# One order of scores and masks in windowed attention, norm roots on one engine, a longer modulation pause and one group of PSUM banks, in a two-layer backbone on one core

## The chip, the cores and the metric

The kernel runs on one core of one Trainium2 chip. The metric is the device time of the whole program in microseconds (us), the median over runs; lower is better.

## The reference, cut to what matters

The reference is a two-layer diffusion backbone over 512 latent tokens with 256 context tokens ahead of them, width 1024, all in fp32. Each layer is half a SwiGLU feed-forward step, a token mixing, and another half step; each of the three is fed by an RMSNorm modulated by shift, scale and gate, which are computed from the conditioning vectors (adaLN, nine vectors per layer, one set for the latent tokens and one for the context).

```python
def ffn_half_step(x, g, shift, scale, gate, wg, wu, wd):
    h = modulate(rmsnorm(x, g), shift, scale)
    return x + 0.5 * gate * swiglu(h, wg, wu, wd)     # widths 1024 -> 2816 -> 1024

# layer 0 mixes by spatial gating beside windowed attention, layer 1 by a recurrent block
def block(args):                      # one block of 128 queries, 8 query heads on 2 key heads
    qj, kj, vj, mj = args             # kj: the blocks before, at and after the queries
    s_loc = jnp.einsum('bqkgd,bnkd->bkgqn', qj, kj).astype(jnp.float32) * scale
    s_loc = jnp.where(mj, s_loc, NEG_INF)             # |key - query| <= 128
    s_ctx = jnp.einsum('bqkgd,bnkd->bkgqn', qj, k_ctx).astype(jnp.float32) * scale
    p = jax.nn.softmax(jnp.concatenate([s_loc, s_ctx, s_sink], axis=-1), axis=-1)
    ...
```

## The kernel before, in words

**Layout.** All activations are held transposed, features on the 128 partitions and 768 tokens (256 context, then 512 latent) along the free axis. Work on tokens goes in two halves of 384, the first and the second half below. Every fp32 product is made of three matmuls on operands split into a high and a low part (`mm3`), issued through the helper at line 121; so almost all matmuls carry the line L121 in the trace, and the tile names tell them apart: `pgu`, `pd` and `seeded` for the feed-forward products, `ps` for projections, norm sums and spreads, `sl` and `sc` for local and context scores, `pt` for transposes of the probabilities, `po` for output projections.

**What sets the order.** Instructions are emitted from Python into one stream per engine; a scheduler behind the program may still bring an instruction that is ready ahead of others of its engine. A planner (`Clock`, with `clk.at`) advances an estimated time with every matmul that is emitted and fires the events that are due: preparing weights (loads on SP's queue, splits into high and low on ScalarE and VectorE, at L198, L201, L228 and L245), the applying of norms, and steps of the modulation.

**Modulation.** `ada_event` (L521) makes one step of the adaLN product each 1.7 us of the planner's time in the first FFN, each 2.5 us in the second and each 4.8 us between them; a step is two updates on VectorE (L496) of a running sum with a loaded piece of the weights (`aw`). It pauses while `bg["on"]` is false. That is set false at L856, ahead of the last down projection of each feed-forward step, and true again when the next norm has been applied to the second half.

**Norms.** When a half of the tokens has its new residual, `stats` (L575) sums the squares with a matmul against ones, and `rsqrt` (L142) takes the reciprocal root of the sums: three VectorE instructions, then three Newton rounds on 128x3 or 128x4 elements. For a second half they run on VectorE with three instructions a round (L150, L152, L153); for a first half on GpSimd with four (L150, L155, L156, L157). `spread` then brings the roots to all partitions with a matmul against the identity, and the norm is applied feature block by feature block. Five first-half norms of this kind are waited for by TensorE: ahead of the mixing of layer 0, ahead of the second FFN of layer 0, ahead of the two FFN steps and the mixing of layer 1.

**PSUM.** The eight PSUM banks are in two groups, six (`psp`) and two (`psx`). `bank()` (L108) goes round all eight, except while `banks["six"]` is set: then it goes round the six, and the two others hold the pair of tiles that stay for a whole run of chunks (`hold`, L764). This pair belongs to the feed-forward chunks made with seven products in place of eight (`seven`, L771): the pair is seeded by copies on ScalarE (L790, L792) and added to by later products. Two chunks, gate and up, make a pair of feature blocks (`gate_up_seven`). The last group of a step makes two of these pairs and then the last down projection (L843 to L856).

**Attention.** A `Unit` is one block of 128 queries, one key head and two query heads; there are 16 over the latent tokens and 8 over the context. `weigh` (L1046) makes for each of the two heads the local scores (three matmuls on 64 rows, as a head has 64 features), then adds the masks of the window's two edges (a bf16 matmul of 128 rows against the identity per edge: one for the outer blocks, two for the inner ones), then takes the row maximum on VectorE; after both heads come the context scores of both in one bank, their maximum, and the exponentials on ScalarE. `turn` transposes the probabilities on TensorE a unit later.

Of the kernel before, what the change touches and what calls it, by code (L numbers as in the profile page):

```python
# [12 lines left out]
F32 = mybir.dt.float32  # L13
# [4 lines left out]
ALU = mybir.AluOpType  # L18
PSUM = bass.MemoryType.PSUM
DRAM = bass.MemoryType.DRAM  # L20

D = 1024
DK = 8
DFF = 2816
NCTX = 256
NX = 512
NT = NCTX + NX
# [62 lines left out]
def hybrid_kernel(ctx: ExitStack, tc: tile.TileContext, a: dict, out: bass.AP):  # L90
# [10 lines left out]
    psp = ctx.enter_context(tc.tile_pool(name="psp", bufs=6, space=PSUM))  # L101
    psx = ctx.enter_context(tc.tile_pool(name="psx", bufs=2, space=PSUM))
# [3 lines left out]
    banks = {"n": 0, "six": False}  # L106

    def bank(name="ps"):  # L108

        banks["n"] = (banks["n"] + 1) % 8  # L110
        if banks["n"] >= 6 and banks["six"]:
            banks["n"] = 0
        if banks["n"] >= 6:
            return psx.tile([128, 512], F32, tag="px", name=name)
        return psp.tile([128, 512], F32, tag="ps", name=name)
# [429 lines left out]
    class Norm:  # L545
# [29 lines left out]
        def stats(self):  # L575
            nt = self.n // 128
            ps = bank()
            for i in range(nt):
                mm(ps[:, i:i + 1], self.ssq[:, i * 128:(i + 1) * 128], ones[:, 0:1], True, True, 4)
            self.r = const.tile([128, 4], F32, tag="rstd" + self.which, name="rstd")  # L580
            rsqrt(ps[:, 0:nt], self.r[:, 0:nt], nt, 1.0 / D, self.which, dve if self.c1 == NT else pool)
# [70 lines left out]
    def ffn(l, j, halves, before, nxt, reserve=(), pre={}):  # L652
# [7 lines left out]
        with tc.tile_pool(name=f"ffn{l}{j}", bufs=4) as fp:  # L660
# [101 lines left out]
            held = {}  # L762

            def hold():  # L764

                banks["six"] = True
                for n in (6, 5):
                    held[n] = psx.tile([128, 512], F32, tag="px", name="seeded")[:, 0:384]
                    mm(held[n], hi[0][:, 0:128], hi[0][:, L], True, True)
# [54 lines left out]
            for gi, (f0, ng, dn) in enumerate(steps):  # L824
# [18 lines left out]
                if saving:  # L843
                    gate_up_seven(f0, G)
                    gate_up_seven(f0 + 2, G)
                    banks.update(six=False, n=5)
# [49 lines left out]
    def even_mixer(before):  # L896
        hi, lo = H
        xd = dp.tile([128, 8, NT], F32, name="xd")
        with ExitStack() as es:
# [140 lines left out]
            class Unit:  # L1040
# [5 lines left out]
                def weigh(self):  # L1046
# [16 lines left out]
                    S = {}  # L1063
                    if kind == "x":
                        k0, k1 = max(0, j - 1), min(4, j + 2)
                        n = (k1 - k0) * 128
                        self.kblocks += [2 + b for b in range(k0, k1)]
                        for hh in range(2):
                            ps = bank("sl")
                            scores(ps[:, 0:n], 2 * p + hh, NCTX + k0 * 128, NCTX + k1 * 128, False)  # L1070
                            edge = [(0, 0)] * (j > 0) + [(n - 128, 1)] * (j < 3)
                            for e, (o, m) in enumerate(edge):
                                mm(ps[:, o:o + 128], identb, masks[:, m], False, e == len(edge) - 1)
                            S[hh] = ps
                            dve.tensor_reduce(st[:, hh, 1:2], ps[:, 0:n], axis=mybir.AxisListType.X, op=ALU.max)
                    pc = bank("sc")
                    for hh in range(2):
                        scores(pc[:, hh * 256:hh * 256 + 256], 2 * p + hh, 0, NCTX, True)
                    dve.tensor_reduce(st[:, :, 0:1], pc.rearrange("p (h n) -> p h n", h=2), axis=mybir.AxisListType.X, op=ALU.max)
# [376 lines left out]
    for cc in range(4):  # L1456
# [4 lines left out]
        if cc == 0:  # L1461
            two = arrive(*TB)
            stream["limit"] = 8
            for i, key in enumerate(pre):
                pre[key] = bank("pre") if i < 2 else psx.tile([128, 512], F32, tag="px", name="pre")
            banks["six"] = True
# [106 lines left out]
```

## Time and profile before

| | |
|---|---|
| median of 3 runs | 2602.93 us (2600.84 to 2604.24) |
| profiled execution, its own time | 2604.11 us |
| its span in the trace | 2602.3 us |
| granted TensorE clock, mean | 0.988 of full speed |
| busy share: PE, PEld, DVE, ACT, POOL | 97%, 91%, 72%, 48%, 9% |
| DMA | 328.46 MB, mean 126 GB/s |

PE is TensorE's matmuls, PEld its weight loads (they overlap the matmuls), DVE is VectorE, ACT is ScalarE, POOL is GpSimd, SP is SyncE, which issues loads. The span is the time from the first to the last instruction of the profiled execution; all starts in the rows are microseconds from its begin. The granted clock is the share of full speed that the chip gave TensorE. A matmul's end is modelled and overlaps the start of the next, so the distance of two starts tells more of its cost than its duration.

### The profile page before, as it was taken

Reading aid. Unit: us, or ns where it says so; the run is one execution under the profiler, and the core shown is the slowest. Engines: PE = TensorE matmul, PEld = TensorE weight load, DVE = VectorE, ACT = ScalarE, POOL = GpSimd, SP = SyncE. Lnnn points to the kernel's source line nnn. Section 1 sums busy time; section 2 is a strip of 40 time slices with the busy share of each in tenths; the row PEclk is TensorE's granted clock in tenths of the full one; section 3 lists DMA queues with packets and bytes.
Section 4 is the critical chain, followed back from the end, with each engine's and each line's share of the span. In section 5 each row is a group of like instructions: output and inputs, shape, how many; then the busy total and the mean of one; then the engine's idle time right before and its main releaser. Section 6 shows DMA issues by size and latency. Waiting matters only on the chain. (4 is left out here: it accounts for less than half of the span.)

```text
span 2602.3 us, 37742 instructions
## 1 busy us (share of the span) xinstructions
PE 2534.7 (97%) x14370; PEld 2356.5 (91%) x14370; DVE 1875.2 (72%) x3635; ACT 1246.4 (48%) x2433; POOL 227.5 (9%) x329
## 2 busy tenths in 40 slices
PE   8999999999999999999999999999999999999998
PEld 5999999999899999999999889999999988988887
DVE  7987987887869697786687978745468898644444
ACT  3344444445555344444454444444545996433322
POOL 0012102200000002102220020121200000000000
PEclk9999999999999999999999999999999999999999
DMA  9357557652103416646675176554642123332221
GB/s 326 113 131 194 156 144 171 152 177 97 49 17 110 139 60 163 152 140 130 146 182 192 48 178 193 159 102 106 138 130 81 51 80 103 108 97 97 90 89 57
DMA packets 248430, 328.46 MB, mean 126 GB/s; under 512 B 19984, under 2 KB 172728, under 8 KB 247736
## 3 DMA queue, kind: packets, MB, share of 16 engines
q1 hardware_dynamic: 213264, 278.69, 33.2%
q0 software_dynamic: 34560, 47.20, 12.3%
q8 instruction: 112, 1.84, 0.3%
q14 instruction: 70, 0.57, 0.1%
q10 hardware_dynamic: 424, 0.15, 0.0%
HBM read 262.04 MB, written 63.96 MB: 125 GB/s over the span
## 5 line engine op out<-in xcount | busy, mean ns | idle before, releaser
L121 PE MATMUL pd<-ghi,w 128*128 128x256 f32 (+2 forms) x2528 | 645.7, 342 | 1.9 <-ACT ghi L135 1.8
L121 PE MATMUL pgu<-hhi,w 128*128 128x384 f32 (+2 forms) x2144 | 594.8, 349 | 0.9 <-ACT hhi L601 0.6
L121 PEld LDWEIGHTS pd<-ghi,w 128*128 128x128 f32 x2528 | 440.0, 188 | 53.9 <-ACT ghi L135 4.7
L121 PE MATMUL pd<-glo,w 128*128 128x512 f32 (+2 forms) x1264 | 431.4, 342 | 0.6 <-DVE glo L136 0.6
L121 PEld LDWEIGHTS pgu<-hhi,w 128*128 128x128 f32 x2144 | 393.0, 189 | 27.6 <-ACT hhi L601 1.3
L121 PE MATMUL pgu<-hlo,w 128*128 128x384 f32 (+2 forms) x1072 | 374.8, 350 | 1.3 <-DVE hlo L607 1.2
L201 DVE TENSOR_TENSOR w<-raw,w 128x512 fp32r<-128x512 f32 x404 | 270.5, 687 | 85.0 <-ACT w L198 79.0
L198 ACT ACTIVATE w<-raw 128x512 fp32r<-128x512 f32 x404 | 244.6, 626 | 181.9 <-PE pd L121 79.3
L496 DVE SCALAR_TENSOR_TENSOR acc<-aw,cs,acc 128x512 f32<-128x512 f32 x392 | 281.1, 745 | 56.3 <-DMA aw<-in_ada_w_dram 55.5
L696 POOL DMA_DIRECT2D kept<-add x240 | 208.9, 910 | 1184.1 <-ACT add L695 1179.2
L228 DVE TENSOR_TENSOR w<-raw,w 128x512 fp32r<-128x512 f32 x348 | 232.2, 687 | 108.2 <-ACT w L245 105.9
L121 PE MATMUL seeded<-form,w 128*128 128x384 f32 x1392 | 263.2, 336 | 5.0 <-ACT seeded L790 3.2
L121 PEld LDWEIGHTS pd<-glo,w 128*128 128x128 f32 x1264 | 237.9, 188 | 27.5 <-DVE glo L136 2.9
L695 ACT ACTIVATE add<-pd,gate 128x256 f32<-128x256 f32 x240 | 138.3, 580 | 245.6 <-PE pd L121 232.5
L121 PE MATMUL seeded<-hhi,w 128*128 128x384 f32 x928 | 247.9, 335 | 3.0 <-DVE uv L798 1.7
L121 PEld LDWEIGHTS seeded<-form,w 128*128 128x128 f32 x1392 | 244.5, 189 | 6.7 <-ACT seeded L790 3.9
L245 ACT ACTIVATE w<-raw 128x512 fp32r<-128x512 f32 x348 | 207.5, 626 | 61.7 <-DVE raw L242 20.2
L121 PEld LDWEIGHTS pgu<-hlo,w 128*128 128x128 f32 x1072 | 202.8, 189 | 15.2 <-DVE hlo L607 2.1
L121 PE MATMUL ps<-hhi,w 128*128 128x384 f32 (+1 forms) x704 | 198.3, 356 | 7.6 <-ACT t L1327 6.3
L121 PEld LDWEIGHTS seeded<-hhi,w 128*128 128x128 f32 x928 | 168.6, 188 | 5.5 <-DVE uv L798 2.7
L121 PE MATMUL seeded<-hlo,w 128*128 128x384 f32 x464 | 155.1, 335 | 0.4 <-DVE hlo L136 0.4
L121 PEld LDWEIGHTS ps<-hhi,w 128*128 128x128 f32 x704 | 132.5, 194 | 15.4 <-ACT t L1327 7.2
(304 smaller groups left out, 3655.3 us busy)
## 6 DMA issues: line engine op xcount, KB each, us to landing
aw<-in_ada_w_dram SPq DMA_DIRECT2D x128, 512.0 KB, 5.3
raw<-in_ffn_w_gate_dram SPq DMA_DIRECT2D x44, 1024.0 KB, 5.4
raw<-in_ffn_w_up_dram SPq DMA_DIRECT2D x44, 1024.0 KB, 5.3
raw<-in_ffn_w_down_dram SPq DMA_DIRECT2D x40, 1024.0 KB, 5.2
kept<-add POOLq DMA_DIRECT2D x120, 256.0 KB, 5.6
kept<-add POOLq DMA_DIRECT2D x120, 128.0 KB, 5.4
x<-kept SPq DMA_DIRECT2D x48, 192.0 KB, 4.2
fw<-in_ada_w_dram SPq DMA_DIRECT2D x16, 512.0 KB, 8.9
```

The lines of the kernel that those rows point to most:

```text
L121: pe.matmul(o, w, x, start=start, stop=stop, skip_group_check=again)
L198: act.activation(tiles[i][:, 0:512], self.raw[:, i * 512:i * 512 + 512], AF.Copy)
L201: dve.tensor_tensor(t[:, 512:1024], self.raw[:, i * 512 - 512:i * 512], t[:, 0:512].bitcast(F32), op=ALU.subtract)
L228: dve.tensor_tensor(l, src[key], h.bitcast(F32), op=ALU.subtract)
L245: act.activation(halves_of(key)[0], src[key], AF.Copy)
L496: dve.scalar_tensor_tensor(acc[:, v, :], w[:, k, :], s, acc[:, v, :], op0=ALU.mult, op1=ALU.add)
L695: act.activation(t, ps[:, 0:c1 - c0], AF.Copy, scale=state["gate"][:, 4 * c + d, v:v + 1])
L696: pool.dma_start(out=saved(l, j)[:, 4 * c + d, c0:c1], in_=t, accum_op=ALU.add)
```

## The change

In `weigh` the context scores and their maximum come first, then the local scores of both heads, then the masks of both heads with their maxima. The Newton rounds of all norms of `stats` go to VectorE. In the last group of a feed-forward step with seven-product chunks the modulation is switched off between the two pairs of feature blocks, in place of after them. The two groups of PSUM banks become one of eight, and the held pair is taken from it.

```diff
--- before.py
+++ after.py
@@ -98,20 +98,11 @@
     wp = ctx.enter_context(tc.tile_pool(name="wp", bufs=SLOTS))
     rp = ctx.enter_context(tc.tile_pool(name="rp", bufs=2))
     tp = ctx.enter_context(tc.tile_pool(name="tp", bufs=8))
-    psp = ctx.enter_context(tc.tile_pool(name="psp", bufs=6, space=PSUM))
-    psx = ctx.enter_context(tc.tile_pool(name="psx", bufs=2, space=PSUM))
+    psp = ctx.enter_context(tc.tile_pool(name="psp", bufs=8, space=PSUM))
     dp = ctx.enter_context(tc.tile_pool(name="dp", bufs=1, space=DRAM))
 
 
-    banks = {"n": 0, "six": False}
-
     def bank(name="ps"):
-
-        banks["n"] = (banks["n"] + 1) % 8
-        if banks["n"] >= 6 and banks["six"]:
-            banks["n"] = 0
-        if banks["n"] >= 6:
-            return psx.tile([128, 512], F32, tag="px", name=name)
         return psp.tile([128, 512], F32, tag="ps", name=name)
 
     def temp(name="t"):
@@ -578,7 +569,7 @@
             for i in range(nt):
                 mm(ps[:, i:i + 1], self.ssq[:, i * 128:(i + 1) * 128], ones[:, 0:1], True, True, 4)
             self.r = const.tile([128, 4], F32, tag="rstd" + self.which, name="rstd")
-            rsqrt(ps[:, 0:nt], self.r[:, 0:nt], nt, 1.0 / D, self.which, dve if self.c1 == NT else pool)
+            rsqrt(ps[:, 0:nt], self.r[:, 0:nt], nt, 1.0 / D, self.which, dve)
 
         def prep_mod(self):
             m = mod(self.l, 3 * self.j + 1)
@@ -763,9 +754,8 @@
 
             def hold():
 
-                banks["six"] = True
                 for n in (6, 5):
-                    held[n] = psx.tile([128, 512], F32, tag="px", name="seeded")[:, 0:384]
+                    held[n] = bank("seeded")[:, 0:384]
                     mm(held[n], hi[0][:, 0:128], hi[0][:, L], True, True)
 
             def seven(ch, emit):
@@ -842,8 +832,8 @@
                     continue
                 if saving:
                     gate_up_seven(f0, G)
+                    bg["on"] = False
                     gate_up_seven(f0 + 2, G)
-                    banks.update(six=False, n=5)
                     for i in range(2):
                         X[i] = xp.tile([128, 4, NT], F32, tag="x", name=f"x{i}")
                     for c0, c1 in halves:
@@ -1061,22 +1051,22 @@
 
                     self.kblocks = [0, 1]
                     S = {}
+                    pc = bank("sc")
+                    for hh in range(2):
+                        scores(pc[:, hh * 256:hh * 256 + 256], 2 * p + hh, 0, NCTX, True)
+                    dve.tensor_reduce(st[:, :, 0:1], pc.rearrange("p (h n) -> p h n", h=2), axis=mybir.AxisListType.X, op=ALU.max)
                     if kind == "x":
                         k0, k1 = max(0, j - 1), min(4, j + 2)
                         n = (k1 - k0) * 128
                         self.kblocks += [2 + b for b in range(k0, k1)]
+                        edge = [(0, 0)] * (j > 0) + [(n - 128, 1)] * (j < 3)
                         for hh in range(2):
-                            ps = bank("sl")
-                            scores(ps[:, 0:n], 2 * p + hh, NCTX + k0 * 128, NCTX + k1 * 128, False)
-                            edge = [(0, 0)] * (j > 0) + [(n - 128, 1)] * (j < 3)
+                            S[hh] = bank("sl")
+                            scores(S[hh][:, 0:n], 2 * p + hh, NCTX + k0 * 128, NCTX + k1 * 128, False)
+                        for hh in range(2):
                             for e, (o, m) in enumerate(edge):
-                                mm(ps[:, o:o + 128], identb, masks[:, m], False, e == len(edge) - 1)
-                            S[hh] = ps
-                            dve.tensor_reduce(st[:, hh, 1:2], ps[:, 0:n], axis=mybir.AxisListType.X, op=ALU.max)
-                    pc = bank("sc")
-                    for hh in range(2):
-                        scores(pc[:, hh * 256:hh * 256 + 256], 2 * p + hh, 0, NCTX, True)
-                    dve.tensor_reduce(st[:, :, 0:1], pc.rearrange("p (h n) -> p h n", h=2), axis=mybir.AxisListType.X, op=ALU.max)
+                                mm(S[hh][:, o:o + 128], identb, masks[:, m], False, e == len(edge) - 1)
+                            dve.tensor_reduce(st[:, hh, 1:2], S[hh][:, 0:n], axis=mybir.AxisListType.X, op=ALU.max)
                     if kind == "x":
                         dve.tensor_tensor(st[:, :, 0:1], st[:, :, 0:1], st[:, :, 1:2], op=ALU.max)
                     dve.tensor_tensor(st[:, :, 0:1], st[:, :, 0:1], sink8[:, h0:h0 + 2].unsqueeze(2), op=ALU.max)
@@ -1461,9 +1451,8 @@
         if cc == 0:
             two = arrive(*TB)
             stream["limit"] = 8
-            for i, key in enumerate(pre):
-                pre[key] = bank("pre") if i < 2 else psx.tile([128, 512], F32, tag="px", name="pre")
-            banks["six"] = True
+            for key in pre:
+                pre[key] = bank("pre")
         for k in ks:
             for (c, f, i), ps in pre.items():
                 mm3(ps[:, 0:384], (wg, wu)[i].w(k, f * 128, f * 128 + 128),
```

## Rows read from the trace of the kernel before

**Rows 1.** The page's part 1: busy time, share of the span, instructions per engine.
```profile
PE 2534.7 (97%) x14370; PEld 2356.5 (91%) x14370; DVE 1875.2 (72%) x3635; ACT 1246.4 (48%) x2433; POOL 227.5 (9%) x329
```

**Rows 2.** Waits of PE: what was waited for, us in total, times, longest.
```profile
PE ps L121 <- POOL rstd L157: 9.0, 5, 2.5
PE ps L121 <- ACT t L1327: 6.3, 3, 3.1
...
PE ps L121 <- DVE ssq L572: 4.5, 3, 1.5
...
PE seeded L121 <- ACT seeded L790: 3.2, 2, 2.4
```

**Rows 3.** Timeline of PE, one-mask unit: start, us, operation, tiles, shapes, [idle before].
```profile
777.33 0.38 PE L121 MATMUL sl<-kv,qh 64*128 64x256 f32 x1
...
777.67 0.28 PE L121 MATMUL sl<-kv,qh 64*128 64x256 f32 x1
777.88 0.23 PE L121 MATMUL sl<-masks,identb 128*128 128x128 bf16 x1
778.04 0.38 PE L121 MATMUL sl<-kv,qh 64*128 64x256 f32 x1
...
778.75 0.38 PE L121 MATMUL sc<-kv,qh 64*128 64x256 f32 x1
778.97 0.28 PE L121 MATMUL sc<-kv,ql 64*128 64x256 f32 x1
...
779.45 0.28 PE L121 MATMUL sc<-kv,qh 64*128 64x256 f32 x1
779.65 0.33 PE L1111 MATMUL pt<-ident,pc 128*128 128x128 f32 x1
```

**Rows 4.** Timeline of PE, a unit with two masks for each head.
```profile
741.33 0.44 PE L121 MATMUL sl<-kv,qh 64*128 64x384 f32 x1
...
742.05 0.28 PE L121 MATMUL sl<-masks,identb 128*128 128x128 bf16 x2
742.27 0.44 PE L121 MATMUL sl<-kv,qh 64*128 64x384 f32 x1
...
744.11 0.44 PE L1111 MATMUL pt<-ident,pc 128*128 128x128 f32 x2
```

**Rows 5.** Timeline of PE, the spreads of four first-half norms and one sum.
```profile
565.71 1.65 PE L121 MATMUL ps<-ident,rstd 128*128 128x128 f32 x6 [2.53 <-POOL rstd L157]
...
884.62 0.93 PE L121 MATMUL ps<-ident,rstd 128*128 128x128 f32 x6 [2.55 <-POOL rstd L157]
...
1421.74 0.80 PE L121 MATMUL ps<-ones,ssq 128*128 128x1 f32 x6 [1.48 <-DVE ssq L572]
...
1427.04 0.94 PE L121 MATMUL ps<-ident,rstd 128*128 128x128 f32 x6 [0.69 <-POOL rstd L157]
...
2210.59 1.22 PE L121 MATMUL ps<-ident,rstd 128*128 128x128 f32 x4 [2.52 <-POOL rstd L157]
```

**Rows 6.** Windows: us, busy of PE, PEld, DVE, ACT, POOL, PEclk, DMA share, GB/s.
```profile
560.00:570.00 10.00, 7.47 (x38) 7.15 (x37) 5.54 (x13) 2.60 (x5) 3.62 (x12) 0.83 0.17 52
```

**Rows 7.** Timeline of POOL, begin of the first root's Newton rounds.
```profile
561.13 0.19 POOL L150 TENSOR_TENSOR rs<-rstd 128x3 f32<-128x3 f32 x1 [77.71 <-DVE rstd L148]
```

**Rows 8.** Timeline of DVE, begin and end of two second-half Newton chains.
```profile
911.77 0.15 DVE L150 TENSOR_TENSOR rs<-rstd 128x3 f32<-128x3 f32 x1
...
917.46 0.15 DVE L153 SCALAR_TENSOR_TENSOR rstd<-rs,rstd 128x3 f32<-128x3 f32 x1
...
1449.50 0.16 DVE L150 TENSOR_TENSOR rs<-rstd 128x3 f32<-128x3 f32 x1
...
1451.07 0.16 DVE L153 SCALAR_TENSOR_TENSOR rstd<-rs,rstd 128x3 f32<-128x3 f32 x1
```

**Rows 9.** Timeline of DVE, a modulation update before the third norm.
```profile
1416.06 0.75 DVE L496 SCALAR_TENSOR_TENSOR acc<-aw,cs,acc 128x512 f32<-128x512 f32 x1 [1.89 <-DMA aw<-in_ada_w_dram]
```

**Rows 10.** Tile aw: engine, operation, duration ns (min/median/max), first and last start.
```profile
L496 DVE SCALAR_TENSOR_TENSOR acc<-aw,cs,acc x392: 724/745/755, 43.4 to 1667.7; 128x512 f32<-128x512 f32 x196
```

## The prediction

> **What bounds the kernel.** I read the page's part 1 first: TensorE is busy 2534.7 of 2602.3 us, 97% of the span, VectorE 72%, ScalarE 48%, GpSimd 9% [rows 1]. TensorE is the bound, and an edit is worth what it takes from TensorE's own work or from the 67.6 us in which it stands idle. Then the waits of TensorE [rows 2]: the longest group is the norm's reciprocal root on GpSimd, 9.0 us in 5 waits; the sums of squares on VectorE add 4.5 us in 3, the gate sigmoids of the odd mixer 6.3 us in 3, the seeding of the held banks 3.2 us in 2. Last the timelines at the lines that the diff touches, and there the windows, since a gap can cost more than itself: in the 10 us around the first root the granted clock is 0.83 [rows 6]. The levels are 2.4 and 1.2 GHz, so 0.17 of 10 us, 1.7 us of work, is lost on top of the wait. Three of the five gaps have such a window (0.83 each, after waits of 2.53, 2.55 and 2.52 us [rows 5]); the two short ones of 0.7 us have not.
>
> **Scores in a row, masks behind them (attention).** There are 16 units over x (4 blocks, 2 key heads, 2 pairs). Before, TensorE does: scores of head 0, its masks, scores of head 1, its masks, context scores of both, then transposes. The scores use 64 rows of the array, masks and transposes 128. The starts in [rows 3] show what a change costs. Within one kind a 256-column matmul takes 0.12 us: the first three scores start at 777.33 and the third at 777.67, so 0.34 for two, and after a mask the first takes 0.22 (778.75 to 778.97); 0.34 less 0.22 is 0.12. The score ahead of a mask takes 0.21 (777.67 to 777.88), that ahead of the transposes 0.20 (779.45 to 779.65): 0.09 extra each. A lone mask takes 0.16 (777.88 to 778.04), two in a row 0.22 [rows 4], so a mask followed by a mask takes 0.06 and one followed by a score 0.10 more. The score after the mask has 0.10 extra too.
> After the change a unit has the 6 context scores, 6 local scores, then 2 or 4 masks, then the transposes. Removed: two entries into masks less the one that stays (0.09), two exits from masks to scores (2 x 0.20), and the exit from scores to transposes (0.09): 0.58 us. Added: the last mask to the transposes, which no row shows. The bounds are 0 (like mask to mask) and 0.10 (like mask to score). So 0.48 to 0.58 per unit; I take 0.53, times 16 = 8.5 us. The unit's block of 2.32 us (777.33 to 779.65), and 2.78 us with two masks per head (741.33 to 744.11 [rows 4]), should become about 1.8 and 2.25.
> In the Trainium skill, "TensorEngine Tiling (Array Packing)", section Key Properties, says that a change of tiling mode, not of the tile, drains TensorE. The trace agrees for 64 to 128 rows, and no run here shows the mask to transpose step; by that rule it would not drain, as both have 128 rows, and the term would be 16 x 0.58 = 9.3 us.
> What hides the rest: the row maxima move. The context maximum comes first, and the two local ones end the block, so the exponentials of a unit start some 0.3 us later; its transposes come only after the next unit's scores and filling matmuls, a unit later (12 us here: three units lie between 741.33 and 777.33 [rows 3, 4]), so TensorE does not see it. Lower bound of the term: the instructions are put in order by a scheduler that may slip other work between the masks; half of it, 4 us.
>
> **Norm roots on VectorE.** Five first-half norms change engine; each loses 12 GpSimd instructions and gains 9 on VectorE. On GpSimd the first chain runs from 561.13 [rows 7] to TensorE's start at 565.71 [rows 5]: 4.6 us. On VectorE a bare chain takes 1.73 us (1449.50 to the end at 1451.23 [rows 8]); with another instruction in every gap 5.84 us (911.77 to 917.61 [rows 8]). These are the two ends: 2.9 us earlier than now, or 1.3 later. Behind the chain on VectorE stand the residual updates and sums of the second half, delayed by 9 x 0.2 = 1.8 us at most; they have that much idle time. Nothing else waits on GpSimd's queue: its accumulating DMAs are all issued by then.
> First norm (565.71): the modulation pauses there after the change, so the bare end is nearer. The wait of 2.53 and the slow clock of 1.7 go, 4.2. But the operands that the next stage reads start only as much earlier as the spread ends: 565.71 + 1.65 = 567.36 becomes 563.18 + 0.93 = 564.11 (0.93 from the second spread [rows 5]), 3.25. I take 3.2.
> Second (884.62, out projection): no pause, so modulation can fill the gaps; the nearest rows are the filled chain, 30 us later [rows 8]. Its eight fillers, five modulation steps and three weight preparations, cost (5.84 - 1.73) / 8 = 0.51 us each. With the five alone the chain takes 4.3 against 4.6: 0.3 gained, the clock still lost. Bounds 4.2 gained to 1.3 lost.
> Third (1427.04) and fourth (what is left of the 9.0, 0.7 too): no modulation near, bare chain: 0.7 each.
> Fifth (2210.59): no modulation is left, but weight preparations fill some gaps; with three, 1.73 + 3 x 0.51 = 3.3 against 4.6: 1.3 gained, a wait of 1.2 stays. The wait of 1.48 at 1421.74 [rows 5] left the clock whole, so the 1.7 go too: 3.0. Bounds 1.3 lost to 4.2 gained.
>
> **Pause of the modulation.** It now stops one pair (two chunks, about 29 us) before the last down projection. Before the third norm a modulation step waits 1.89 us for its DMA at 1416.06 with the updates queued behind it [rows 9], and TensorE then waits 1.48 us for the sum of squares at 1421.74 [rows 5]; the fourth norm, when modulation is over, has no such wait. So 1.5 gained; at worst 0, if the update that follows is late anyway. Some 17 steps in the first FFN (one per 1.7 us) and 12 in the second (one per 2.5) move later, with their loads on SP's queue; the last step moves from 1667.7 [rows 10] by about 29 x 2.5 = 73 us to 1740, 200 us ahead of the fourth norm and in a stretch where VectorE has room. In the pair itself VectorE's work only shrinks. No norm comes to wait for its modulation.
>
> **One group of banks.** Eight banks go round in either form and held banks leave six; I count zero. Bounds: the 6.3 us of sigmoid waits [rows 2] gained, or a new wait at each held pair (a rival).
>
> Sum: 8.5 + 3.2 + 0.3 + 0.7 + 0.7 + 3.0 + 1.5 = 17.9 us. The profiled execution took 2604.1 us (span 2602.3, the rest lies around it and stays), 1.2 above the median of 2602.9. So 2586.2 for the profile and **2585.0 us** as median. A measurement of this kernel can tell about 0.2%, 5.2 us, from no change.
>
> **Rivals.**
> Filled chains: VectorE's order puts modulation steps, whose data were loaded before the pause, into every gap of the chain. For it: the chain from 911.77. Against: the bare one from 1449.50 [rows 8]. Price: 1.3 lost at the first, second and third, the fourth and fifth as forecast: 8.5 + 1.5 - 3.9 + 0.7 + 3.0 = 9.8, so 2593.1. Chance 0.17.
> The masks do not stay together: at the first x units the timeline shows scores of two units and products interleaved. Then 0 to 4 of the 8.5 are left: 2589.5 to 2593.5. Chance 0.08, that of a change that doesn't do what it says.
> Slower: the held pair shares the group with all others, so the banks that a chunk's first two products take are no longer apart from the seeded ones, and a product waits for an evacuation. There are 58 such chunks (18, 20, 20). Its price is the wait per chunk; the seeding wait averages 1.6 us where it occurs [rows 2]. From 0.31 us per chunk, 17.9 us in all, it eats the whole gain; at 0.6 it gives 2585.0 + 34.8 = 2619.8. For it: this wait exists. Against: it occurs twice in 58, and six free banks are the number as before. Chance 0.06.
>
> **How the numbers follow.** Forecast 0.65 (2578 to 2592), filled chains 0.17, masks apart 0.08, slower 0.06, sigmoid waits also gone 0.04 (2585.0 - 6.3 = 2578.7). Best ends of the terms (masks 16 x 0.58): 9.3 + 3.2 + 4.2 + 1.4 + 4.2 + 1.5 = 23.8, so 2579.1; half of the masks' term with filled chains: 9.8 - 4.5 = 5.3, so 2597.6. Range 2577 to 2598. Faster by more than 0.2% means below 2597.7: the forecast, the sigmoid case, most of masks apart and filled chains: 0.87. Same 0.07, slower 0.06.
>
> **What would show it.** Right: blocks of 1.8 and 2.25 us per unit; no wait of TensorE for GpSimd's root, chains under 4 us on VectorE, clock 1.00 around the first and fifth spread; no wait on the sum of squares ahead of the third norm; last modulation step after 1700 us. Wrong: a wait of TensorE on a VectorE root of 2 us or more at a first half, masks apart from each other, or new waits at the seeded banks.

## The result, and the profile after

The changed kernel took 2579.87 us in the median of 4 runs (2577.0 to 2584.91), the kernel before 2601.89 us in 4; the ratio is 0.9918, with a 95% interval of 0.9899 to 0.9936. That is 22.0 us less, where 17.9 were forecast. The profiled execution took 2580.57 us, with a span of 2578.8 us.

Part 1 of the page after; it answers to [rows 1]:

```profile
PE 2522.0 (98%) x14370; PEld 2354.4 (91%) x14370; DVE 1883.5 (73%) x3680; ACT 1247.0 (48%) x2433; POOL 210.2 (8%) x269
```

GpSimd has 60 instructions less (five norms by twelve) and VectorE 45 more (five by nine), as the diff says. TensorE's busy time fell by 12.7 us and its idle time from 67.6 to 56.8 us.

Waits of TensorE after, to be read against [rows 2]:

```profile
PE ps L112 <- ACT t L1317: 6.3, 3, 3.1
...
PE ps L112 <- DVE ssq L563: 4.4, 4, 1.6
PE ps L112 <- DVE red L497: 3.5, 1, 3.5
...
PE seeded L112 <- ACT seeded L780: 2.6, 1, 2.6
PE pt L1101 <- ACT pc L1080: 2.5, 2, 1.4
...
PE pt L1101 <- DVE rs_z L141: 2.2, 1, 2.2
...
PE ps L112 <- DVE rstd L144: 1.0, 1, 1.0
```

No wait for GpSimd's root is left, and one of 1.0 us for VectorE's. The sigmoid waits stand as they were. The wait for a modulation sum (`red`) in the first 120 us was 0.7 us before and is 3.5, and transposes, which waited once for 0.9 us, wait three times for 4.7 in all.

Timeline of TensorE after, the two kinds of unit; it answers to [rows 3, 4]:

```profile
743.30 0.39 PE L112 MATMUL sc<-kv,qh 64*128 64x256 f32 x1
...
745.28 0.40 PE L112 MATMUL sl<-masks,identb 128*128 128x128 bf16 x4
745.51 0.28 PE L1101 MATMUL pt<-ident,pc 128*128 128x128 f32 x1
...
777.44 0.38 PE L112 MATMUL sc<-kv,qh 64*128 64x256 f32 x1
...
778.86 0.28 PE L112 MATMUL sl<-kv,qh 64*128 64x256 f32 x1
779.07 0.29 PE L112 MATMUL sl<-masks,identb 128*128 128x128 bf16 x2
779.19 0.28 PE L1101 MATMUL pt<-ident,pc 128*128 128x128 f32 x1
```

The blocks take 2.21 us (743.30 to 745.51) and 1.75 us (777.44 to 779.19); before they took 2.78 and 2.32. The two masks take 0.12 us up to the first transpose, 0.06 each, so going from a mask to a transpose costs nothing. The Trainium skill ("TensorEngine Tiling (Array Packing)", Key Properties) says that a change of the tiling mode, and not of the tile alone, drains TensorE. By that rule the step from mask to transpose is free and a unit saves 0.58 us; the trace agrees, with 0.57.

Timeline of TensorE after, spreads of first-half norms, and two waits of the second halves; it answers to [rows 5]:

```profile
567.72 0.83 PE L112 MATMUL ps<-ident,rstd 128*128 128x128 f32 x6
...
588.69 1.44 PE L112 MATMUL ps<-ones,ssq 128*128 128x1 f32 x6 [1.58 <-DVE ssq L563]
...
879.39 0.83 PE L112 MATMUL ps<-ident,rstd 128*128 128x128 f32 x6
...
909.17 0.94 PE L112 MATMUL ps<-ident,rstd 128*128 128x128 f32 x6 [0.95 <-DVE rstd L144]
...
1409.87 0.83 PE L112 MATMUL ps<-ident,rstd 128*128 128x128 f32 x6
...
2189.66 0.71 PE L112 MATMUL ps<-ident,rstd 128*128 128x128 f32 x4
```

None of the first halves' spreads waits (the fourth, at 1939.50, doesn't either). Behind the first norm there is a wait that was not there before, of the second half's sum at 588.69. TensorE's order differs here: 3192 matmuls stand ahead of the sum in this trace and 3212 in the trace of before, so it comes 20 matmuls sooner.

Windows after, behind the first norm (columns as in [rows 6]):

```profile
585.00:595.00 10.00, 7.89 (x26) 6.98 (x27) 7.21 (x28) 1.43 (x3) 0.00 (x0) 0.52 0.74 239
```

The slow clock of the first norm is not gone, it came later: 0.52 in these 10 us. The instructions on tile `aw` after, against [rows 10]:

```profile
L487 DVE SCALAR_TENSOR_TENSOR acc<-aw,cs,acc x392: 722/746/754, 44.3 to 1715.1; 128x512 f32<-128x512 f32 x196
```

**Where the time went, by stage.** Both traces hold all 14370 matmuls. The table gives, for the same count of matmuls, how much later (+) or earlier (-) than in the trace of before TensorE gets through each stage; the first column is the end of the stage in the trace of before. The columns behind "after" are runs told of below: the order alone, the roots alone, the pause alone, the one group alone, all but the one group (two groups), and the shifted modulation.

```
to us   what lies there                 after  order  roots  pause  group  two gr. shifted
 121    start, first modulation          +4.3   +3.7   +2.1   +0.4   +2.9   -0.1   -0.2
 545    first FFN                        +0.4   -1.4   -1.4   +0.2   -1.7   -1.7   +4.5
 606    first norm                       -0.8   +0.1   -5.7   -4.0   +2.6   -4.3   -0.6
 677    mixer, first units over x        +1.8   -0.9    0.0   +3.2   +0.7   +1.4   -0.6
 802    twelve units over x              -6.8   -6.8    0.0    0.0    0.0   -6.8    0.0
 848    last units, gating               -1.0   +0.4   -0.6   -2.6   -0.1   -0.5   -2.7
 934    second norm, both halves         -9.1   -2.6   -3.5   -7.3    0.0   -9.3   -8.3
1414    second FFN                       -3.0   +0.2   -0.7   -3.4   -0.5   -5.0   -4.5
1475    third norm                       -3.1   +2.8   +3.1   -1.5   +3.6   -2.1   -1.6
2207    FFN, fourth norm, odd mixer      -2.6   +0.2   -1.2   -2.0   -1.6   -3.3   +4.4
2229    fifth norm                       -3.4   +0.1   -4.0   -1.5   -1.4   -4.0   -1.4
2592    last FFN                         -0.1    0.0   +0.2   -0.1   -0.1   +0.1    0.0
        sum                             -23.6   -4.4  -11.7  -18.6   +4.3  -35.5  -11.1
```

Each column is one execution, and in a few places the order of TensorE's matmuls differs between the columns. The first line and the stages of the third norm move by 3 to 4 us from one execution to another (below), so totals are read from the medians of the timed runs, and the table only for places.

### The profile page after: what moved, and what is told of

The parts are those of the page before. It is cut to its first block, busy times and chain, and to the rows that moved or that the text cites. A ratio compares the mean times of both kernels' runs of the same rounds, so it can differ in the third digit from the quotient of the medians.

```text
span 2578.8 us, 37727 instructions
## 1 busy us (share of the span) xinstructions
PE 2522.0 (98%) x14370; PEld 2354.4 (91%) x14370; DVE 1883.5 (73%) x3680; ACT 1247.0 (48%) x2433; POOL 210.2 (8%) x269
## 4 chain that ended last, share of the span: by engine, by line
PE 88%; DVE 6%; ACT 3%; DMA 2%; issue 1%; SPq 0%; ACTq 0%; DVEq 0%
PE pd L112 26%; PE pgu L112 25%; PE seeded L112 18%; PE ps L112 11%; PE po L112 4%; PE pv L112 2%; PE sc L112 1%; PE pt L1101 1%; PE sl L112 1%; DVE w L192 1%; PE pre L112 1%; DMA raw<-in_ffn_w_down_dram 1%; ACT w L189 1%; DVE hlo L598 0%; DMA fw<-in_ada_w_dram 0%
```

## The experiments

All were timed in five rounds beside the kernel before, whose medians there were 2601.24, 2601.75, 2603.29 and 2602.44 us. A gain "in the median" is against the one of the same group of runs.

**The four parts, each alone.** Each has its own part of the diff shown above and nothing else. Of the diffs below only the lines that tell the runs apart are shown.

The order of scores and masks:

> Only the new order of scores and masks, all else as before. Theory: the entries and exits between 64-row scores and 128-row masks are what is saved, 0.57 us in each of 16 units (blocks of 1.75 and 2.21 us instead of 2.32 and 2.78), 9.1 us; and the later row maxima cost some of it where the first units over x follow each other without cover, as waits of TensorE for the exponentials of 1 to 1.4 us at two places. Total: 5 to 7 us faster. Rival A: the later maxima cost nothing and the waits of the changed kernel in the first units come from the one group of banks; then the transposes wait as before and the total is 9 us faster. Rival B: blocks are shorter but the units are bound by VectorE or ScalarE; then within 2 us of before.

Measured: 2592.42 us, ratio 0.9964 (0.9952 to 0.9977), 8.8 us faster. The median is that of rival A, 9 us. In the table the twelve units from 677 to 802 give 6.8 us, 12 x 0.57; around them it gains 0.9 and loses 0.4. The waits of 1 to 1.4 us at the first units that the theory expected are not there; they are 0.5 us. The order is worth its blocks.

The roots:

> Only the norm roots on VectorE, modulation pausing as before. Theory: the waits of TensorE for GpSimd's roots go, but at the first norm modulation steps fill the chain, so a wait for the root stays there; 3 to 4 us each are won at the second and the fifth norm, 0.7 at the third and fourth. Total: 7 to 9 us faster. Rival A: the first norm's wait only moves to the sum of squares of the second half, the clock drop with it, whatever the modulation does, so nothing at the first norm, and the same 7 to 9. Rival B: filled chains at the first three norms; 0 to 3 us faster.

Measured: 2592.42 us, 0.9961 (0.9947 to 0.9974), 8.8 us faster, the total of the theory and of rival A. But rival A has nothing at the first norm, where the table has 5.7, and the theory has a wait for the root there of which 0.22 us stayed. The chain there is filled as the theory had it (5.84 us, 562.36 to 568.19, four modulation updates in it); but from the begin of the sum to its spread there are 51 matmuls in TensorE's order in this run, and 27 before, so TensorE has more other work in between. At the second norm waits stayed. Timelines of TensorE and of VectorE in this run:

```profile
880.47 0.94 PE L121 MATMUL ps<-ident,rstd 128*128 128x128 f32 x6 [1.91 <-DVE rstd L153]
...
909.70 0.93 PE L121 MATMUL ps<-ident,rstd 128*128 128x128 f32 x6 [2.64 <-DVE rstd L153]
```

```profile
874.97 0.15 DVE L150 TENSOR_TENSOR rs<-rstd 128x3 f32<-128x3 f32 x1
875.03 0.74 DVE L496 SCALAR_TENSOR_TENSOR acc<-aw,cs,acc 128x512 f32<-128x512 f32 x1
...
880.26 0.15 DVE L153 SCALAR_TENSOR_TENSOR rstd<-rs,rstd 128x3 f32<-128x3 f32 x1
```

Here the nine instructions took 5.44 us (874.97 to 880.41), with another instruction in every gap: the prediction's filled chain. Of the eight fillers two are modulation updates and four weight preparations. In the changed kernel the chain holds a single residual update and takes 2.13 us (VectorE after, its first and last instruction):

```profile
876.44 0.16 DVE L141 TENSOR_TENSOR rs<-rstd 128x3 f32<-128x3 f32 x1
...
878.41 0.16 DVE L144 SCALAR_TENSOR_TENSOR rstd<-rs,rstd 128x3 f32<-128x3 f32 x1
```

So something else in the change took the fillers away, the weight preparations with the updates.

The pause:

> Only the earlier pause of the modulation. Theory: the wait of 1.48 us for the sum of squares before the third norm goes; nothing else of weight on TensorE's path changes, 1 to 2 us faster. Rival: the shifted modulation steps also free the chain of the second half's root at the second FFN of layer 0 (before: a wait of 2.81 us and slow clock after it) and the waits for copies and weights in the 250 us behind it; then 5 to 9 us faster.

Measured: 2585.02 us, 0.9934 (0.9915 to 0.9953), 16.2 us faster, more than either had. The rival's place is right: 7.3 us at the second norm, 3.4 in the FFN behind it. Where the modulation's updates lie shows why. Windows of VectorE for line L496 alone (us, busy and count, granted clock, DMA share, GB/s), before:

```profile
530.00:580.00 50.00, 8.91 (x12) 0.97 0.60 176
...
870.00:920.00 50.00, 7.33 (x10) 0.93 0.29 96
```

and with the pause alone:

```profile
530.00:580.00 50.00, 0.00 (x0) 1.00 0.54 150
...
870.00:920.00 50.00, 2.07 (x3) 1.00 0.30 94
```

The updates have left the first norm, where the pause is, and also most of the second norm, 300 us behind it: all later ones run later. They come in groups of 14. The group that lies across the second norm before starts at 879 us, and with the pause alone at 975; the two groups ahead of it start 75 and 76 us later than before. A step is one update (not two, as the words on the kernel before have it), and the steps left out at one per 1.7 us are made up at one per 4.8 us; for some 17 steps that is an estimated 82 us. At the second norm it is thus not a pause but a shift. The second half's spread there, before:

```profile
917.67 1.65 PE L121 MATMUL ps<-ident,rstd 128*128 128x128 f32 x6 [2.81 <-DVE rstd L153]
```

With the pause alone it waits 0.95 us, and the first half's 1.50 in place of 2.55.

The one group of banks:

> Only the one group of PSUM banks. Theory: nothing on average, within 2 us, and the waits for the odd mixer's sigmoids (6.3 us in 3) stay. Rival A: the more freely chosen banks take away the waits of the held pair for ScalarE's copies in the second FFN of layer 0 (1.13 and 0.63 us before) and those for weights; 3 to 5 us faster. Rival B: the later start of the modulation's first sums in the changed kernel (3.5 us of wait instead of 0.7 near 112 us) comes from the banks taken at the start; then 3 to 4 us slower.

Measured: 2610.49 us, 1.0034 (1.0021 to 1.0046), 9.2 us slower. The theory and rival A fall. Of rival B the direction is right; of its place, below (its own wait for the modulation sum is 1.3 us in this run, and 3.4 in the run with the order alone, which has two groups). Timeline of TensorE with the one group alone, two waits that the kernel before has not:

```profile
588.51 1.44 PE L112 MATMUL ps<-ones,ssq 128*128 128x1 f32 x6 [1.58 <-DVE ssq L563]
...
660.22 0.33 PE L1100 MATMUL pt<-ident,pc 128*128 128x128 f32 x1 [0.96 <-ACT pc L1079]
```

The changed kernel has them too: 1.58 us at 588.69, and 1.39 and 1.14 us of transposes near 665.

**All but the one group.**

> The changed kernel with the two groups of PSUM banks of before (order, roots and pause stay). Theory: the one group costs what it cost alone, 9 us (waits of the transposes in the first units over x, at the second half's sum behind the first norm), so this is 6 to 10 us faster than the changed kernel, 28 to 32 us faster than before. Rival: with the pause the held banks and the transposes no longer meet, and the one group costs nothing there: within 2 us of the changed kernel.

Measured: 2569.71 us (4 runs, 2568.58 to 2572.57), 0.9882 (0.9865 to 0.9899): 32.0 us faster than before and, by the two ratios against before, some 9 us faster than the changed kernel. It beats both. The theory holds: the one group costs what it cost alone.

**Only the first of the two pauses.**

```diff
+                    bg["on"] = bg["on"] and (l, j) != (0, 0)
                     gate_up_seven(f0 + 2, G)
```

> Only the earlier pause in the first feed-forward step of layer 0, not in the second one. Theory: the pause of the first step brings nearly all, as it shifts every later modulation step: its sixteen updates no longer meet the first norm (2 to 4 us), the next ones no longer meet both roots of the second norm (9 us), and the chunks of the second step see fewer late weights (2 to 4 us); 12 to 15 us faster in all, with a wait for the sum of squares before the third norm again. Rival: the gain of the pause sits in the second step, where modulation is densest; then 3 to 5 us faster.

Measured: 2593.03 us, 0.9967 (0.9956 to 0.9979), 8.7 us faster, between the theory and the rival. The first pause brings half. Its profile has the second norm's spreads at waits of 1.50 and 0.95 us, the same as with both pauses, so that place is the first pause's. Where the second pause brings its 7 us I have not placed: between the two traces no stage differs by more than 2.4 us (the second FFN).

**Order and pause, roots on GpSimd, two groups.**

> Order and pause alone, roots on GpSimd and two groups of banks as before. To be read against the run that has the roots on VectorE besides. Theory: with the pause in, the first norm's wait for GpSimd is 0.4 us and the second's 1.5 us, so the roots on VectorE are worth only those, the fifth norm's 3 to 4 us and two waits of 0.7 us: this is 5 to 7 us slower than that run, 24 to 26 us faster than before. Rival: the gains of roots and pause are of the same waits, then 3 us slower than that run; or they add up, then 10 us.

Measured: 2579.42 us, 0.9913 (0.9897 to 0.9928), 22.3 us faster than before and 9.7 slower than with the roots on VectorE. The second rival holds: the roots bring nearly 10 us with the pause (and the order) and 8.8 without. The two sums are not made in the same places. By the traces the roots give 0.3 us at the first norm, 1.9 at the second and 2.6 at the fifth with the pause, and 5.7, 3.5 and 4.0 without it; with the pause 4.2 us of the difference lie in the first two FFNs, where no root is, and why is not shown.

**The shift without the pause.**

```diff
-            ada_step()
+            if clk.t > 250e3 and bg["skip"]:
+                bg["skip"] -= 1
+            else:
+                ada_step()
```

> No earlier pause, all else as before too; the modulation leaves out eight steps (sixteen updates) once, 250 us into the first step by the planner's time, and so runs that much later from there on. Theory: the wait at the first norm stays as before (2.5 us for the root on GpSimd, with its slow clock), but the second norm's two roots are free of modulation as with the pause, 8 to 10 us faster around 870 to 925 us, and 8 to 13 us faster in all. Rival: the pause itself is what counts, where it lies; then within 3 us of before.

Measured: 2591.96 us, 0.996 (0.9944 to 0.9976), 9.8 us faster. The counter starts at 8, and a step is one update, so it left out eight updates, not sixteen. Windows of VectorE for L496 alone:

```profile
530.00:580.00 50.00, 6.55 (x9) 1.00 0.65 190
...
870.00:920.00 50.00, 0.00 (x0) 1.00 0.24 83
```

No pause comes earlier here, and the second norm is free of updates all the same; the stage to 934 gives 8.3 us, and the second half's spread (at 911.60) waits for nothing. That the shift, not the pause, brings the gain at the second norm is shown. On the first norm I was wrong: its updates now end ahead of the sum, and its root is waited for only 0.42 us. The 4.5 us that this run loses in the first FFN hold a wait of TensorE of 5.56 us at 495.45 for a product that VectorE reads out (`uv`), from a cause that is not shown.

This run also shows why an update near a root on GpSimd costs so much. Timeline of GpSimd, then of VectorE, in the first norm of this run:

```profile
565.43 0.19 POOL L150 TENSOR_TENSOR rs<-rstd 128x3 f32<-128x3 f32 x1
...
566.80 0.45 POOL L155 TENSOR_TENSOR rs<-rs 128x3 f32<-128x3 f32 x1
```

```profile
565.37 0.62 DVE L652 SCALAR_TENSOR_TENSOR x<-pd,gate,x 128x384 f32<-128x384 f32 x1 [1.13 <-PE pd L121]
...
566.65 0.56 DVE L575 TENSOR_TENSOR ssq<-ssq,sq 128x384 f32<-128x384 f32 x1 [0.65 <-ACT sq L569]
```

And in the kernel before, GpSimd, then VectorE:

```profile
561.68 0.76 POOL L156 TENSOR_SCALAR rs<-rs 128x3 f32<-128x3 f32 x1
```

```profile
561.64 0.74 DVE L496 SCALAR_TENSOR_TENSOR acc<-aw,cs,acc 128x512 f32<-128x512 f32 x1
```

A small GpSimd instruction takes 0.19 us beside a VectorE update that reads one operand from PSUM (565.37), and ends with the VectorE instruction where that reads two tiles of SBUF: 566.80 + 0.45 against 566.65 + 0.56, 561.68 + 0.76 against 561.64 + 0.74. The Trainium skill ("SBUF — State Buffer", Who interferes with whom) says that the two engines share a port pair under an exclusive lock, and that a VectorE instruction with two SBUF inputs contends for it with a GpSimd instruction that reads SBUF; these rows agree, with 0.45 and 0.76 us in place of 0.19. So modulation updates lengthened the GpSimd chains as well: 4.54 us at the first norm before (561.13 to 565.67), 3.49 here (564.33 to 567.82).

**One group in part.** The two groups are given up at a point and opened as one, or the reverse:

```diff
+    def regroup(one):
+        groups.close()
+        P.update(one=one, psp=groups.enter_context(tc.tile_pool(name="pso" if one else "psp", bufs=8 if one else 6, space=PSUM)))
+        if not one:
+            P["psx"] = groups.enter_context(tc.tile_pool(name="psx", bufs=2, space=PSUM))
...
             def hold():
+                if (l, j) == (0, 0):
+                    regroup(False)
```

That is the first run; the second has (0, 1) and regroup(True) in these lines. The order, the roots and the pause are those of the changed kernel in both, and in the two runs that follow.

> Order, roots and pause as changed; one group of eight banks only until the first pair of tiles is held in the first feed-forward step (some 200 us in), two groups of six and two from there on. To be read between the run with two groups throughout (2569.7 us) and the changed kernel with one group throughout (2579.9). Theory: the cost of the one group sits in the middle, at the first norm and the first units of attention, where banks go to whichever tile comes next; then this is within 2 us of the run with two groups. Rival: it sits in the start, where the changed kernel's profile has 4.5 us more by 121 us; then 3 to 6 us above that run.

> The same, but two groups until the first pair of tiles is held in the second feed-forward step of layer 0 (about 930 us in), one group from there on. Theory: behind that point the one group costs 0 to 3 us against the run with two groups throughout (2569.7 us), as the products of the held pairs find a free bank in either form. Rival, the one of the prediction: the held pairs and the products that share their group wait for each other; then 5 us or more above that run.

Measured: 2575.6 us, 0.9896 (0.987 to 0.9922), and 2575.88 us, 0.9902 (0.9882 to 0.9921). Both medians lie some 6 us above the run with two groups (3.6 and 5.2 by the ratios), and both intervals overlap its own, so neither pair of expectations is decided. What reopening alone costs, without any stage in one group:

```diff
             def hold():
+                regroup(False)
```

> Order, roots and pause as changed and two groups throughout, but both groups are given up and opened again where the pair of tiles is first held, in each of the three feed-forward steps with seven-product chunks. This is what the two runs with one group in part do once each besides. Theory: each reopening makes TensorE wait 1 to 2 us for the banks to be read out, 3 to 6 us in all above the run with two groups (2569.7 us); so of the 6 us that the two runs with one group in part lost, 1 to 3 each are the reopening and the rest is the one group. Rival: reopening costs nothing, within 1 us of that run; then all of it is the one group.

Measured: 2574.26 us, 0.9888 (0.9872 to 0.9905), 4.6 us above in the median, 0.6 thousandths in the ratio. The medians leave the price open; the traces show waits. TensorE where the pair is taken, at the third reopening of this run and at the one reopening of the run with one group late (`g` is read out of a bank on VectorE):

```profile
1459.27 0.69 PE L131 MATMUL pgu<-hhi,w 128*128 128x384 f32 x1 [3.60 <-DVE g L692]
```

```profile
930.51 0.61 PE L131 MATMUL seeded<-hhi 128*128 128x384 f32 x2 [1.94 <-DVE g L692]
```

The run with two groups waits at neither place. In this run the first reopening has a wait of 0.47 us and the second none. So part of what the run with one group late lost is the reopening and not the one group.

The run also settles something else. Timelines of TensorE at the first modulation sum, in this run and then in the first run with two groups throughout:

```profile
112.82 0.59 PE L131 MATMUL ps<-red,quarters 128*128 128x64 f32 x2 [4.14 <-DVE red L516]
```

```profile
110.01 0.43 PE L121 MATMUL ps<-red,quarters 128*128 128x64 f32 x2 [0.90 <-DVE red L506]
```

Up to that point both have two groups, yet the waits are 4.14 and 0.90 us. The 4.3 us that the changed kernel's profile lost by 121 us are therefore no proof against the one group; rival B of the run with the one group alone falls as far as it rested on them. Where the 9 us of the one group sit stays open. By the table 3 to 4 of them lie between 545 and 677 us (alone +2.6 and +0.7; in the changed kernel against two groups 3.5 and 0.4), at the two waits shown. But the run with one group at the start, which has two groups by then, also loses 4.3 us there against the run with two groups throughout, so this place isn't shown either; how long the clock stays low there differs between runs with two groups (last section). One trace of the form can be seen in TensorE's order: ahead of the second half's sum of the first norm stand 3192 matmuls in the two runs with one group throughout, where it waits 1.58 us, and 3196 in the runs with two groups and fewer updates at the first norm, where it waits 0.94 to 1.06. Another is a transpose that waits 2.19 us (at 821.57, changed kernel) and 1.82 for `rs_z`, in those two runs alone; but the stage to 848 is no slower in them.

**A later resumption.** Two groups, and:

```diff
-    bg.update(on=True, every=4800.0)
+    bg.update(on=False, hold=True, every=4800.0)
+    clk.at(110e3, lambda: bg.update(on=True, hold=False))
```

> The run with two groups (2569.7 us), and the modulation stays off for 110 us more by the planner's time when the first feed-forward step is done. Theory: in the runs with the pause the resumed modulation meets the first units of attention over x (a wait of 1.2 us and slow clock there, 1.5 to 4.8 us lost against before by 677 us); without it there 1 to 4 us faster than the run with two groups. Rival: the later steps then meet the second norm's roots, or are forced all at once where they are needed; then up to 9 us slower than that run.

Measured: 2580.75 us, 0.9932 (0.9909 to 0.9954), 11 us slower than the run with two groups in the median. The theory's gain is there: by 677 us this run gained 1.9 us from the stage before, where that run lost 1.4. The rival takes it back several times. Windows of VectorE for L496, and timeline of TensorE, both of this run:

```profile
870.00:920.00 50.00, 5.13 (x7) 0.97 0.29 92
```

```profile
873.60 0.93 PE L121 MATMUL ps<-ident,rstd 128*128 128x128 f32 x6 [2.29 <-DVE rstd L153]
...
902.54 0.93 PE L121 MATMUL ps<-ident,rstd 128*128 128x128 f32 x6 [2.36 <-DVE rstd L153]
...
964.82 0.69 PE L121 MATMUL ps<-red,quarters 128*128 128x64 f32 x2 [3.07 <-DVE red L506]
```

Seven updates are back at the second norm and its spreads wait again. The stage to 934 gives 3.3 us in place of 9.3. The shift works in both directions.

## Why the prediction was right, and where it was not

The total is inside the range and near the forecast, and the two terms forecast with some 8 us each came out, the order by its mechanism, the roots only in their sum. But the other two terms were far off, in opposite directions, and that 17.9 came so near to 22.0 is in good part luck: alone, the parts gave 8.8, 8.8, 16.2 and -9.2 us where 8.5, 7.9, 1.5 and 0 were forecast.

**Scores and masks, 8.5 us: right in its main step.** The blocks came out at 1.75 and 2.21 us against 1.8 and 2.25. The 0.53 of a unit is 0.57: the unknown last step costs nothing, and the middle between the bounds was the wrong choice by 0.04. Alone it measured 8.8 us. That TensorE does not see the later maxima holds for the twelve units of the middle, where the whole 0.57 arrives. At the last units it does not: there the pause alone gains 2.6 us and pause and order together 1.6 on GpSimd's roots, and transposes wait for exponentials 2.22 us in that run and 0.45 with the pause alone. Near 665 us, where they wait 1.39 and 1.14 us in the changed kernel, no transpose waits more than 0.96 us in a run with two groups.

**Roots, 7.9 us: right in the sum, wrong in the places.** Nearly bare chains stand where no update is near: 564.71 to 566.88 at the first norm after, 2.17 us, near the forecast's 1.73. First norm, 3.2: TensorE did win 4.1 us there by 575 us and lost 3.3 again by 606, as it waited for the second half's sum, 20 matmuls sooner in its order than before, and the clock fell to 0.52; the prediction counted only to the start of the next stage and took TensorE's order as fixed. With two groups 4.3 stayed. Second norm, 0.3: the change brought 9.1 us in this stage. Fourth norm, 0.7: the wait went and 0.2 us came of it, since the second half's sum then waits 1.48 us, as it did before. Third norm, 0.7: the spread waits no more, but this stage changes by 3 us between runs that leave it alone (+2.8 with the order), so it can't be told. Fifth norm, 3.0: it measured 3.4, and 4.0 with the roots alone and with two groups (runs that leave it alone moved there by +0.1 to -1.5). The size is right, but not for the reason given: the chain after takes 4.20 us (2185.40 to 2189.60) where 3.3 were forecast, and the wait of 1.2 that should have stayed is gone, as from the begin of the sum to the spread there are 48 matmuls, and 34 before.

**Pause, 1.5 us (16.2 alone): the step that failed.** "No norm comes to wait for its modulation" was right, the last update moved from 1667.7 to 1715.1 us (forecast 1740), and the wait for the sum ahead of the third norm is gone. But the step priced the pause only where it lies, and there it left out the first norm: the pause alone brought 4.0 us there by the table, with GpSimd's chain no longer held up by updates. The modulation is one long queue with a fixed pace, so a pause moves all that follows, and the stage to price was every later one in which an update stood in a chain that TensorE waits for. The rows for it were at hand: the filled chain of [rows 8] at 911.77 holds five updates, and the text even priced it, for the wrong part of the change. It took the fillers as given.

**One group, 0 us: wrong.** It costs 9 us. The rival with 0.06 had the direction, but its place was the held pair, and there the waits for the seeding copies did not grow (2.6 us in one wait after, 3.2 in two before [rows 2]). From 961 us on, behind its reopening, the run with one group late loses 2.6 us against the run with two groups, one execution each; two feed-forward steps with held pairs lie in that stretch. Counting banks was not enough: eight are eight in either form. Why the form matters is not shown; it changes TensorE's order in places, and what that is worth was not measured.

**The rivals.** Filled chains, 0.17: shown in the run with the roots alone, at the first norm (where TensorE waited 0.22 us for them) and the second, and again with the later resumption at the second, and absent from the change as a whole only because the pause moved the fillers. Masks apart: did not occur; in all 16 units of the changed kernel's trace they stand together. Sigmoid waits: still 6.3 us in 3.

## What to carry to other kernels

Background work that runs at a fixed pace has a phase. Before pricing a pause or a resumption, list the places behind it where its instructions stand in a chain that the bound engine waits for, and ask which of them the shift empties or fills; here that brought 7 to 8 us at one norm, and cost 6 of them again when the shift was wrong. The order of the bound engine's instructions is not fixed either: compare how many stand ahead of a wait before and after. Take parts of a change one by one even if the sum is good: this one was 22 us faster with a part in it that cost 9.

## What the runs showed of the hardware

The same waits can bring very different slow stretches of TensorE. In the shifted run and in the run with two groups the second half's sum waits 0.94 us each behind the first norm, after earlier waits of 0.58 to 0.61 us. The windows right behind it, of the shifted run and of the run with two groups:

```profile
585.00:595.00 10.00, 8.99 (x29) 7.99 (x29) 7.47 (x29) 1.51 (x4) 0.00 (x0) 0.50 0.71 225
```

```profile
585.00:595.00 10.00, 10.00 (x62) 10.00 (x61) 8.57 (x27) 4.93 (x11) 0.00 (x0) 1.00 0.64 206
```

One ran this whole stretch at 0.50 of the clock, the lower of the two levels, the other at 1.00, having fallen to 0.83 in the 10 us before. The run with the reopening alone had waits of 0.58, 0.61, 0.42 and 1.05 us there and a clock of 1.00 throughout. So a slow clock of 1.7 us per wait, as the prediction took it, is one outcome of several. What decides between them I could not see.

A VectorE instruction that reads two SBUF tiles holds up a small GpSimd instruction beside it to its own end, 0.19 us becoming 0.45 to 0.76.
